# Third weight unit asked for four pairs sooner, one store for a tile's sums, loads ahead of stores, another order of the first inputs

## The chip, the cores and the metric

The kernel runs on one core of a Trainium2 chip. The metric is the time of one execution on the device in microseconds (us). The kernel before took 2228.83, 2224.96 and 2224.57 us in three runs, a median of 2224.96 us.

## What is computed

One layer of a hybrid encoder on x of 2048 rows by 1024 columns, in float32:

```python
h    = rmsnorm(x, norm_w)                       # row by row
proj = h @ w_in                                 # 1024 -> 10 groups of 1024 columns: q, ffwd, fbwd, i, ga, u, v, gb, ma, mb
y_a  = hgrn2(q, ffwd, fbwd, i, ga)              # two gated linear scans, 8 heads, norm, SiLU gate
y_b  = gelu(u) * (W_s @ layernorm(gelu(v)) + b) * silu(gb)
out  = rmsnorm(x + (sigmoid(ma)*(y_a @ w_proj_a) + sigmoid(mb)*(y_b @ w_proj_b)) @ w_out, final_norm_w)
```

The part that the change touches is the very first: h from x, and h times the 1024 columns of `w_in` that make `i`.

## The kernel before, in words

**Numbers in two halves.** A float32 operand is held as two float16 tensors, a high half and a low half (the rest). A product is three float16 products: high by high, high by low, low by high. These are the three matmuls of lines 218, 219 and 220, repeated for the eight slices of 128 of the depth.

**x.** The 2048 rows are eight pairs of two tiles of 128 rows. `x_pair(n)` makes pair n in four steps: ACT squares both tiles as they lie in `in_x` (L280, which also sums each row), POOL makes 1/sqrt of the mean and puts it on the diagonal of two 128x128 tiles (L283 to L286), PE multiplies a matrix of ones by these diagonals (L290), which spreads each row's factor over all partitions, DVE multiplies the transposed columns of x by it (L296, four times for each half of the depth), ACT rounds to the high half (L300) and DVE makes the low half (L301). Rows come by L263, transposed columns by L267. Two pairs fill one of the four `xT` tiles, which is also stored (`store(b)`, L384: two stores of 1 MB).

**Weights of i.** They come in four units of 256 columns, 1 MB each. `halves` (called through `load`) makes one: DMA of `wraw` (L188), squares on ACT (L192), a cast to bfloat16 on POOL (L196), a matmul with ones on PE, here called the norm (L200, into the one-bank tile `misc`), a power of two from it on DVE (`pow2`, L142 to L147), then for each half the high half on ACT (L207) and the low half on DVE (L208). Line 192 writes its squares, which nobody reads, into the unit's own low half.

**Pairs of i.** `i_pair(hp, n)` multiplies pair n of x by unit hp: 48 matmuls, here written (hp, n), and ACT empties the result (L448). Units 0 and 1 are run through while x is still being made, in the order of the list `seq`: (0,0) (1,0) (0,1) (1,1) (0,2) (0,3) (1,2) (1,3) (0,4) (0,5) (1,4) (1,5) (0,6) (0,7). The table `beside` says what is issued in the middle and after each of them. The pairs (1,6) and (1,7) follow as `i_late`, in `i_stage(2)`, then (2,0) to (2,7), then `i_stage(3)` with (3,0) to (3,7), then the stage `values()`. In `front()` unit 2 (the third unit) is loaded after `x_stage` has been written:

```python
self.x_stage(xr)
...
self.plan_units()
last = self.i_stage(2, self.unit(self.w_in, C_I + 2 * U, ahead=0), wu3)
```

**Sums of x.** A later stage needs four sums S1, S3, S2, S4 of blocks of x. `x_parts(p, k)` makes one of eight tiles of them, each in two steps of `self.parts`: DVE adds (L963), then ACT and DVE make the halves (L955, L956) in a tile `st`, and four stores of 256 KB put them into four arrays (L958). `st` is the single buffer `xst`, or for two of the eight the former row buffer `xt2` (shown as `xt`).

**What sets the order.** The framework's scheduler puts the instructions of each engine in one order, and each engine runs its own in that order. It follows roughly the order in which Python wrote them, with `tc.high_priority` and `tc.issue_after` for a few at the start, but an instruction can land behind some that were written later: the norm of unit 2 is written ahead of (1,6) and stands behind (1,7). All DMAs of this part are issued by the SP queue in order. They share eight semaphores in rotation, so that an issue also waits until the DMA eight issues earlier has landed. `self.make(at)` issues what a plan of units (`plan_units`) has due by the number `at`: loads, squares and scales of the weights of the `values()` stage (L1011 to L1070, L1084).

## Time and profile before

| | |
|---|---|
| median of three runs | 2224.96 us |
| the profiled execution | 2224.79 us |
| its span | 2223.1 us |
| PE busy | 2164.2 us (97%) |
| DVE, ACT, POOL busy | 1664.5, 1347.8, 334.5 us |
| first matmul of unit 2's norm (L200) | at 126.42 us |

The profile is of one execution. Idle time before an instruction stands in brackets behind it with what ended it. The lowest rate of the clock that the throttle granted to PE is 0.50, the highest 1.00; a column of the windows gives it for each stretch.

### The profile page before, as it was taken

The numbers are of one execution on the slowest core, as the hardware profiler recorded it, in microseconds if no ns is written. First come the engines' busy times: TensorE is split into PE (matmuls) and PEld (weight loads), VectorE is DVE, ScalarE is ACT, GpSimd is POOL, SyncE is SP. The second block draws the span as 40 slices with busy tenths as digits, with TensorE's granted clock in tenths as the row PEclk, the third lists the DMA queues.
The fourth block names the chain that finished last, engine by engine and source line by source line (L and its number), as shares of the span: only waits on it lengthen the run. The fifth ranks groups of instructions, "written<-read, shape, count | busy, mean of one in ns | idle before, by whom it ended". The sixth has DMA issues, their size and how long they took to land.

```text
span 2223.1 us, 35062 instructions
## 1 busy us (share of the span) xinstructions
PE 2164.2 (97%) x12654; PEld 1216.8 (55%) x12654; DVE 1664.5 (75%) x3063; ACT 1347.8 (61%) x2740; POOL 334.5 (15%) x526
## 2 busy tenths in 40 slices
PE   8979999999999999999899999999999999999998
PEld 6868444566666666666454544444445544444444
DVE  6867876688999989989677775588874744687764
ACT  6466876676877877867465564676764622344442
POOL 1125743002402202203100000000000000000011
PEclk9989999999999999999999999999999999999999
DMA  8886996768678668776742223779756675777643
GB/s 318 320 292 263 364 398 243 225 208 218 188 216 248 196 167 258 220 201 192 239 147 95 83 98 123 273 288 324 287 174 220 214 252 179 274 259 285 251 160 104
DMA packets 269449, 503.92 MB, mean 227 GB/s; under 512 B 92880, under 2 KB 154576, under 8 KB 245584
## 3 DMA queue, kind: packets, MB, share of 16 engines
q1 hardware_dynamic: 246080, 459.36, 62.2%
q10 hardware_dynamic: 23184, 42.22, 5.1%
q8 instruction: 101, 1.65, 0.3%
q14 instruction: 84, 0.69, 0.1%
HBM read 317.74 MB, written 166.99 MB: 218 GB/s over the span
## 4 chain that ended last, share of the span: by engine, by line
PE 47%; issue 3%; DVE 0%; ACT 0%; POOL 0%; POOLq 0%; ACTq 0%; DVEq 0%
PE bank L1161 46%; PE px L1491 1%; PE px L1795 0%; DVE seven L1061 0%; ACT seven L1060 0%; DVE zs L1197 0%; ACT tmp L1011 0%; POOL wsb L1016 0%; PE px L1068 0%; DVE tmp L1030 0%; DVE zs L2017 0%; POOLq L2289 0%; ACT zs L2036 0%; DVE raw L1030 0%; POOL rstd L2029 0%
## 5 line engine op out<-in xcount | busy, mean ns | idle before, releaser
L1161 PEld LDWEIGHTS <-seven 128*128 128x128 f16 x7404 | 722.6, 100 | 765.2 <-issue 7.9
L1161 PE MATMUL bank<-xT,seven 128*128 128x512 f16 x4116 | 971.4, 379 | 4.2 <-ACT zs L594 2.5
L1161 PE MATMUL bank<-seven 128*128 128x512 f16 (+1 forms) x2028 | 436.0, 378 | 0.7 <-DVE zs L2017 0.7
L1161 PE MATMUL bank<-xs,seven 128*128 128x512 f16 x1260 | 282.2, 379 | 0.0
L1197 DVE SCALAR_TENSOR_TENSOR zs<-bank,us,zs 128x512 f32<-128x512 f32 x192 | 142.5, 744 | 90.0 <-PE bank L1161 64.2
L1109 ACT ACTIVATE zs<-bank,us 128x512 f32<-128x512 f32 x192 | 130.1, 680 | 106.3 <-PE bank L1161 100.6
L1164 PEld LDWEIGHTS sc<-ff,kt 128*128 128x128 f32 x684 | 130.0, 190 | 47.8
L1205 ACT ACTIVATE zs<-zs 128x512 f32<-128x512 f32 x144 | 90.0, 626 | 99.8 <-DVE zs L1197 87.0
L1161 PE MATMUL bank<-seven,xT 128*128 128x512 f16 x672 | 146.3, 379 | 1.2 <-DVE zs L1197 1.2
L218 PE MATMUL pin<-wsplit,xT 128*128 128x256 f16 x512 | 142.2, 279 | 4.9 <-ACT wsplit L207 4.9
L1061 DVE SCALAR_TENSOR_TENSOR seven<-raw,ws,seven 128x1024 f16<-128x1024 f32 x80 | 109.4, 1395 | 49.6 <-ACT seven L1060 48.9
L220 PE MATMUL pin<-wsplit,xT 128*128 128x256 f16 x512 | 142.0, 278 | 1.1 <-DVE xT L301 1.0
L219 PE MATMUL pin<-wsplit,xT 128*128 128x256 f16 x512 | 142.2, 278 | 0.7 <-DVE wsplit L208 0.7
L1109 ACT ACTIVATE zs<-bank,su 128x512 f32<-128x512 f32 x72 | 49.0, 682 | 144.0 <-PE bank L1161 131.6
L839 ACT ACTIVATE q<-ff,e 128x64 f32<-128x64 f32 x512 | 131.5, 336 | 1.6 <-issue 0.4
L1164 PE MATMUL sc<-ff,kt 128*128 128x64 f32 (+1 forms) x684 | 119.2, 256 | 0.0
L1161 PEld LDWEIGHTS <-xT 128*128 128x128 f16 x672 | 64.6, 98 | 77.3 <-issue 1.5
L1197 DVE SCALAR_TENSOR_TENSOR zs<-bank,su,zs 128x512 f32<-128x512 f32 x72 | 53.8, 747 | 55.5 <-PE bank L1161 44.6
L1060 ACT ACTIVATE seven<-raw,ws 128x1024 f16<-128x1024 f32 x80 | 88.5, 1137 | 5.3 <-DMA kept<-seven 2.5
L1061 DVE SCALAR_TENSOR_TENSOR seven<-tmp,ws,seven 128x768 f16<-128x768 f32 x80 | 80.5, 1035 | 10.8 <-ACT seven L1060 10.4
L915 DVE SCALAR_TENSOR_TENSOR st<-st,e,pu 128x128 f32<-128x128 f32 x224 | 75.7, 338 | 5.4 <-PE pu L907 4.3
L1575 ACT ACTIVATE zs<-zs 128x512 f32<-128x512 f32 x64 | 40.0, 625 | 55.5 <-DVE zs L1963 39.3
(270 smaller groups left out, 3207.7 us busy)
## 6 DMA issues: line engine op xcount, KB each, us to landing
xT<-x SPq DMA_DIRECT2D x71, 1024.0 KB, 7.1
raw<-in_w_in_dram SPq DMA_DIRECT2D x38, 1024.0 KB, 7.3
seven<-kept SPq DMA_DIRECT2D x15, 1792.0 KB, 9.2
kept<-seven SPq DMA_DIRECT2D x16, 1024.0 KB, 5.2
kept<-seven SPq DMA_DIRECT2D x16, 768.0 KB, 6.1
v<-v SPq DMA_DIRECT2D x20, 512.0 KB, 5.3
x<-xT SPq DMA_DIRECT2D x8, 1024.0 KB, 5.8
v<-zs SPq DMA_DIRECT2D x32, 256.0 KB, 8.5
```

The lines of the kernel that those rows point to most:

```text
L218: nc.tensor.matmul(ps, lh(k), rh(k), start=start and k == 0, stop=False, skip_group_check=len(ks) < KT)
L219: nc.tensor.matmul(ps, lh(k), rl(k), start=False, stop=False, skip_group_check=len(ks) < KT)
L220: nc.tensor.matmul(ps, ll(k), rh(k), start=False, stop=k == KT - 1, skip_group_check=len(ks) < KT)
L839: self.nc.scalar.activation(out=q0[:, at], in_=ff[:, at], func=AF.Copy, scale=e8[:, n, b:b + 1])
L915: nc.vector.scalar_tensor_tensor(out=sn, in0=st, scalar=e8[:, n, last:last + 1], in1=pu[:, n, :], op0=ALU.mult, op1=ALU.add)
L1060: nc.scalar.activation(out=out[0], in_=src, func=AF.Copy, scale=s)
L1061: nc.vector.scalar_tensor_tensor(out=out[1], in0=src, scalar=s, in1=out[0], op0=ALU.mult, op1=ALU.subtract)
L1109: self.reads["act"] = self.nc.scalar.activation(out=t, in_=ps, func=AF.Copy, scale=su)
L1161: nc.tensor.matmul(ps, lhs(x, k), rhs(y, k), start=start and not (k or n), stop=k == 3 and n == 2, skip_group_check=True)
L1164: self.fill.pop(0)()
L1197: self.reads["dve"] = self.nc.vector.scalar_tensor_tensor(out=more, in0=ps, scalar=su, in1=more, op0=ALU.mult, op1=ALU.add)
L1205: self.nc.scalar.activation(out=out, in_=more, func=func)
```

## The change

1. **Third unit.** `third()`, in the middle of the pair at entry 10 of `seq`, (1,4), loads unit 2 (DMA, squares, cast); the rest of it (norm, power of two, halves) is written where it was, by `unit()` after `x_stage`. The squares of this unit go into a free piece of a lent buffer (`junk`) and no longer into the unit's low half, which has the place of a unit that PE still reads.
2. **One store a tile.** The four sums lie in one array `x_sums_d[p]`, and `x_parts` stores its tile with one DMA of 1 MB; the old names are views of it.
3. **Loads ahead of stores.** The loads of x's pairs 4 to 7 are issued one or two pairs of `seq` sooner, and the four `store(b)` are issued after the entries 6, 7, 9 and 12 of `seq` where it was 3, 4, 8 and 10.
4. **First inputs.** Unit 0's norm is written after x's first high half; unit 1's norm and scaling come in the middle of the first pair's matmuls (`proj_tm` with `by_quads`), not in their first quarter; the spreading matmul L290 is ordered behind the one of line 102, and the first step of pair 1 behind the high half of unit 0 and not behind its squares.
5. In `i_stage(2)` the plan's work is issued before `i_late`'s pair and not after it.

```diff
@@ scale_x
-            nc.tensor.matmul(pb, self.ones[0:1, :], m1, start=True, stop=True)
+            self.spread = nc.tensor.matmul(pb, self.ones[0:1, :], m1, start=True, stop=True)
@@ halves(self, w, c0, junk=None)
         for h in range(2):
-            self.w_square = nc.scalar.activation(out=quads(wt[:, 1], h), in_=quads(raw, h), func=AF.Square,
-                                                 accum_out=ss[:, h:h + 1])
+            out = quads(wt[:, 1], h) if junk is None else junk.rearrange("p (a n) -> p a n", a=2)
+            nc.scalar.activation(out=out, in_=quads(raw, h), func=AF.Square, accum_out=ss[:, h:h + 1])
@@ proj_tm
-                if j and between and not m:
+                if between and (j and m is None or m and not j):
                     between()
@@ x_pair
-        nc.tensor.matmul(r.rearrange("p (n t) -> p n t", t=P), self.ones, diag, start=True, stop=True)
+        with self.tc.issue_after(self.spread.ins):
+            nc.tensor.matmul(r.rearrange("p (n t) -> p n t", t=P), self.ones, diag, start=True, stop=True)
@@ x_stage
             next(pairs[0])
-            next(wi)
+            next(pairs[0])
+            hi = self.x_hi
             busy(6, self.raws[0][:, 0, 1, 1, 0:P])
-            next(pairs[0])
-            unit(0, partial(next, wi))
+            with tc.issue_after(hi.ins):
+                next(wi)
+                unit(0, partial(next, wi))
...
+        def third():
+            got = self.load(*self.todo[0], junk=lent[1][:, 3072:].bitcast(F16))
+            self.made.append((self.todo.pop(0), got))
...
-            with tc.issue_after(self.w_square.ins):
+            with tc.issue_after(self.w_hi.ins):
                 next(pairs[n])
-                  3: (go(3, 2), go(3, 2) + fetch(4) + [partial(store, 0)]),
-                  4: (part, part + go(4) + fetch(5) + [partial(store, 1)]), 5: (go(4, 2), go(4, 2) + go(5)),
-                  6: (go(5, 2), go(5, 2) + fetch(6)), 7: (part + go(6) + fetch(7), part + [self.decays]),
-                  8: (go(6, 2), go(6, 2) + go(7) + [partial(store, 2)]), 9: (go(7, 2), go(7, 2)),
-                  10: (part, part + [partial(store, 3)]), 11: (part, part), 12: (part, part), 13: (part, part)}
+                  3: (go(3, 2), go(3, 2) + fetch(5) + go(4) + [partial(self.x_load, 6)]),
+                  4: (part, part + go(5) + [partial(rows, 6), partial(self.x_load, 7)]),
+                  5: (go(4, 2), go(4, 2) + [partial(rows, 7)] + go(6)),
+                  6: (go(5, 2), go(5, 2) + go(7) + [partial(store, 0)]),
+                  7: (part, part + [self.decays, partial(store, 1)]),
+                  8: (go(6, 2), go(6, 2)), 9: (go(7, 2), go(7, 2) + [partial(store, 2)]),
+                  10: (part + [third], part), 11: (part, part), 12: (part, part + [partial(store, 3)]), 13: (part, part)}
@@ i_stage
             for n, f in enumerate(self.i_late):
+                self.make(2 * n - 36)
                 f()
-                self.make(2 * n - 36)
@@ x_parts
-        for n, part in enumerate((S1, S3, S2, S4)):
-            nc.sync.dma_start(out=self.x_d[p][part][:, k], in_=st[:, n])
+        nc.sync.dma_start(out=self.x_sums_d[p][:, :, k], in_=st)
```

The instructions of each engine in their order show what this moves. On PE, the norm of unit 2 before, between the last matmul of (1,7) (L220) and the first of (2,0) (L218):

```order
L220 LDWEIGHTS xT
L220 MATMUL pin<-wsplit,xT 128x256
L200 LDWEIGHTS ones_70
L200 MATMUL misc<-wsb,ones_70 128x1
L200 LDWEIGHTS ones_70
L200 MATMUL misc<-wsb,ones_70 128x1
L218 LDWEIGHTS xT
L218 MATMUL pin<-wsplit,xT 128x256
```

With the change the norm stands two pairs sooner, between (0,7) and (1,6), and 96 matmuls lie between it and (2,0). The norm of unit 3 (the fourth unit) stands inside (2,4), 16 matmuls from its start; before it stood right behind (2,3).

On ACT with the change, from the squares of unit 2 (L193, which was L192), through its high halves (L207), to the squares of unit 3 (the last row); L459 empties the pairs, L966 makes sums of x (it was L955), L1021 and L1070 belong to the weights of the next stage:

```order
L193 ACTIVATE lent,wss<-wraw 128x1024
L966 ACTIVATE xt_261<-xraw 128x512
L966 ACTIVATE xt_261<-lent 128x3x512
L459 ACTIVATE vt<-pin 128x512
L966 ACTIVATE xst<-xraw 128x512
L207 ACTIVATE wsplit<-wraw,ws 128x2x512 x2
L966 ACTIVATE xst<-lent 128x3x512
L459 ACTIVATE vt<-pin 128x512 x2
L966 ACTIVATE xst<-xkept 128x512
L966 ACTIVATE xst<-lent 128x3x512
L459 ACTIVATE vt<-pin 128x512
```

The high halves of unit 2, which stood behind all the sums of x but one, now stand between the two conversions of the sixth tile of sums. After these rows come, on ACT, six squares of the next weights (L1021), the conversions of the eighth tile of sums, two scalings (L1070) and then the squares of unit 3:

```order
L459 ACTIVATE vt<-pin 128x512
L966 ACTIVATE xst<-xkept 128x512
L966 ACTIVATE xst<-lent 128x3x512
L1070 ACTIVATE seven<-raw,ws_1687 128x1024 x2
L193 ACTIVATE wsplit,wss<-wraw 128x2x512 x2
```

Before, the squares of unit 3 came behind the eighth tile's conversions too, with one square pair of L1011 between them and no scaling.

On SP with the change, the stretch with unit 2's load (L188); L385 stores xT, L968 the sums, L466 the results of i:

```order
L466 DMA i_2_151<-vt 128x1024
L385 DMA x_0_143<-xT 128x4096
L385 DMA x_2_144<-xT 128x4096
L188 DMA wraw<-in_w_in_dram 128x2048
L968 DMA x_sums_147<-xt_261 512x1x1024
L466 DMA i_2_155<-vt 128x1024
L968 DMA x_sums_147<-xst 512x1x1024
L385 DMA x_7_146<-xT 128x4096
L968 DMA x_sums_148<-xt_261 512x1x1024
```

Before, the same load stood behind six tiles of sums:

```order
L455 DMA i_3_158<-vt 128x1024
L958 DMA x_1_148<-xst 128x1024
L958 DMA x_4_151<-xst 128x1024
L958 DMA x_5_152<-xst 128x1024
L958 DMA x_6_153<-xst 128x1024
L188 DMA wraw<-in_w_in_dram 128x2048
L1084 DMA raw<-in_w_in_dram 128x2048
```

It moved ahead of six of the eight stores of sums.

More of the change, by code (lines that the diff above doesn't have):

```diff
@@ L170, in step, with load @@
             self.made.append((self.todo[0], self.load(*self.todo.pop(0))))
-    def load(self, w, c0):
-        halves = self.halves(w, c0)
+    def load(self, w, c0, junk=None):
+        halves = self.halves(w, c0, junk)
         next(halves)
@@ L182, in load, with halves @@
         return rest
-    def halves(self, w, c0):
+    def halves(self, w, c0, junk=None):
         nc, sm = self.nc, self.sm
@@ L206, in halves @@
         for h in range(2):
-            nc.scalar.activation(out=quads(wt[:, 0], h), in_=quads(raw, h), func=AF.Copy, scale=s)
+            self.w_hi = nc.scalar.activation(out=quads(wt[:, 0], h), in_=quads(raw, h), func=AF.Copy, scale=s)
             nc.vector.scalar_tensor_tensor(out=quads(wt[:, 1], h), in0=quads(raw, h), scalar=s, in1=quads(wt[:, 0], h),
@@ L399, in x_stage @@
             next(pairs[0])
-            next(wi)
+            next(pairs[0])
+            hi = self.x_hi
             busy(6, self.raws[0][:, 0, 1, 1, 0:P])
-            next(pairs[0])
-            unit(0, partial(next, wi))
+            with tc.issue_after(hi.ins):
+                next(wi)
+                unit(0, partial(next, wi))
             next(pairs[0])
             next(pairs[0])
-        with tc.issue_after(self.x_hi.ins):
+        with tc.issue_after(hi.ins):
             wi = self.load(*self.todo[0])
@@ L414, in first @@
         def first(n):
-            with tc.issue_after(self.w_square.ins):
+            with tc.issue_after(self.w_hi.ins):
                 next(pairs[n])
-        beside = {0: ([partial(unit, 1, wi), partial(first, 1)], fetch(3)), 1: (go(1, 4), go(2)), 2: (go(2, 2), go(2, 2) + go(3)),
-                  3: (go(3, 2), go(3, 2) + fetch(4) + [partial(store, 0)]),
-                  4: (part, part + go(4) + fetch(5) + [partial(store, 1)]), 5: (go(4, 2), go(4, 2) + go(5)),
-                  6: (go(5, 2), go(5, 2) + fetch(6)), 7: (part + go(6) + fetch(7), part + [self.decays]),
-                  8: (go(6, 2), go(6, 2) + go(7) + [partial(store, 2)]), 9: (go(7, 2), go(7, 2)),
-                  10: (part, part + [partial(store, 3)]), 11: (part, part), 12: (part, part), 13: (part, part)}
+        beside = {0: ([partial(unit, 1, wi), partial(first, 1)], fetch(3)), 1: (go(1, 4), go(2)),
+                  2: (go(2, 2), go(2, 2) + go(3) + fetch(4)),
+                  3: (go(3, 2), go(3, 2) + fetch(5) + go(4) + [partial(self.x_load, 6)]),
[5 more added lines that the diff above has]
+                  10: (part + [third], part), 11: (part, part), 12: (part, part + [partial(store, 3)]), 13: (part, part)}
         for m, (hp, n) in enumerate(seq):
@@ L2219, in run @@
         self.kept, self.zscale, self.zsums, self.rot = {}, {}, {}, [(0, 1, 2), (0, 1, 2)]
-        self.x_d = [[self.dram.tile([P, 4, 2, SEG], F16, name=f"x_{p}_{c}") for c in range(8)] for p in range(2)]
+        self.x_d = [[self.dram.tile([P, 4, 2, SEG], F16, name=f"x_{p}_{c}") if c in (A11, A12, A21, A22) else None
+                     for c in range(8)] for p in range(2)]
+        self.x_sums_d = [self.dram.tile([P, 4, 4, 2, SEG], F16, name=f"x_sums_{p}") for p in range(2)]
+        for p in range(2):
+            for n, part in enumerate((S1, S3, S2, S4)):
+                self.x_d[p][part] = self.x_sums_d[p][:, n]
         self.i_d = [[self.dram.tile([P, 4, U], F32, name=f"i_{hp}_{b}") for b in range(NSEG)] for hp in range(2)]
```

## The prediction

> **What bounds the kernel now.** I read the page's busy times first, then the windows of three stretches, then the waits of PE in the first stretch, row by row.
>
> ```profile
> span 2223.1 us, 35062 instructions
> PE 2164.2 (97%) x12654; PEld 1216.8 (55%) x12654; DVE 1664.5 (75%) x3063; ACT 1347.8 (61%) x2740; POOL 334.5 (15%) x526
> 0.00:140.00 140.00, 110.23 (x889) 94.03 (x890) 100.84 (x167) 74.98 (x105) 24.92 (x38) 0.89 0.86 322
> 140.00:350.00 210.00, 209.86 (x1368) 130.43 (x1366) 161.16 (x230) 159.36 (x243) 108.19 (x73) 1.00 0.84 329
> 350.00:2223.10 1873.10, 1844.08 (x10402) 992.39 (x10400) 1402.52 (x2667) 1113.47 (x2393) 201.37 (x415) 1.00 0.64 208
> ```
>
> A window's row gives its bounds and length, the busy time of PE, weight loads, DVE, ACT and POOL, the granted clock of PE, the DMA engines' share and GB/s. PE is busy 97% of the span. In the first 140 us it idles 140.00 - 110.23 = 29.8 us and its clock averages 0.89; from 140 to 350 it idles 0.14 us in 210. So the kernel is bound by PE, and its start is not. The change touches only the start, so what it saves there shifts everything after, as long as the PE-bound stretch stays full.
>
> Where the start loses time:
>
> ```profile
> 27.08 0.70 PE L290 MATMUL xps<-lent,ones 128*128 128x256 f32 x2 [3.03 <-POOL lent L286]
> 75.25 0.70 PE L290 MATMUL xps<-lent,ones 128*128 128x256 f32 x2 [2.77 <-POOL lent L286]
> 83.78 0.70 PE L290 MATMUL xps<-lent,ones 128*128 128x256 f32 x2 [1.36 <-POOL lent L286]
> 126.42 0.19 PE L200 MATMUL misc<-wsb,ones 128*128 128x1 bf16 x2 [9.18 <-POOL wsb L196]
> 131.48 1.23 PE L218 MATMUL pin<-wsplit,xT 128*128 128x256 f16 x5 [4.88 <-ACT wsplit L207]
> 133.40 0.37 PE L219 MATMUL pin<-wsplit,xT 128*128 128x256 f16 x1 [0.69 <-DVE wsplit L208]
> 76.10:79.50 3.40, 3.40 (x18) 2.43 (x17) 3.11 (x8) 2.06 (x4) 0.00 (x0) 0.50 1.02 401
> 82.90:86.30 3.40, 2.52 (x21) 2.17 (x22) 2.14 (x6) 0.47 (x1) 0.83 (x1) 1.00 0.98 405
> 131.50:137.50 6.00, 5.30 (x25) 3.62 (x25) 6.00 (x4) 4.00 (x6) 2.28 (x2) 0.50 1.00 418
> ```
>
> The brackets hold the idle time and its releaser. Unit 2's preparation costs PE 9.18 + 4.88 + 0.69 = 14.8 us, and then 6.0 us at half clock, worth 3.0. The factors of x's pairs 6 and 7 cost 2.77 + 1.36 = 4.1, and 3.4 us at half clock, worth 1.7. Pair 1's factors cost 3.03.
>
> **Third unit.** Its load was asked at 116.61 and its squares ended the wait:
>
> ```profile
> 116.61 0.45 SPq L188 DMA_DIRECT2D wraw<-in_w_in_dram  x1
> 123.65 1.06 ACT L192 ACTIVATE wsplit<-wraw 128x1024 f16<-128x1024 f32 x1 [0.58 <-DMA wraw<-in_w_in_dram]
> 85.83 0.60 ACT L448 ACTIVATE vt<-pin 128x512 f32<-128x512 f32 x1 [3.23 <-PE pin L220]
> 91.07 0.60 ACT L448 ACTIVATE vt<-pin 128x512 f32<-128x512 f32 x1 [0.96 <-PE pin L220]
> 96.31 0.60 ACT L448 ACTIVATE vt<-pin 128x512 f32<-128x512 f32 x1 [2.67 <-PE pin L220]
> wraw<-in_w_in_dram SPq DMA_DIRECT2D x4, 1024.0 KB, 8.5
> 130.28 2.19 ACT L207 ACTIVATE wsplit<-wraw,ws 128x1024 f16<-128x1024 f32 x2 [2.93 <-DVE ws L147]
> 107.26 1.76 DVE L956 TENSOR_TENSOR xt<-lent,xt 128x1536 f16<-128x1536 f32 x1 [1.60 <-ACT xt L955]
> 109.05 0.69 DVE L963 TENSOR_TENSOR lent<-xraw 128x512 f32<-128x512 f32 x1
> 43.70:109.02 65.32, 61.19 (x535) 53.38 (x534) 53.63 (x89) 33.34 (x44) 6.39 (x9) 0.97 0.84 319
> DVE xraw L296 <- PE xps L290: 4.5, 3, 2.0
> ```
>
> A pair takes 96.31 - 91.07 = 5.24 us. I place all that follows 6.7 us sooner than before (the next two parts: 4.1 + 1.7 + 0.9). The load now stands on SP behind the store of (0,5), emptied at 85.83 - 6.7 = 79.1; with three issues it is asked at about 82, and by its median of 8.5 us is there at 90.5. ACT takes the squares around (0,6)'s emptying, ending at about 97.5. (0,7) ends two pairs after (1,5), at 96.3 - 6.7 + 2 x 5.24 = 100.0: the norm waits for nothing, with 2 us to spare. (1,6) and (1,7) then cover 10.5 us, to 110.5.
>
> In that cover DVE is the narrow place. Its power of two stands behind the low halves of the fifth tile of sums, which ended at 109.02. Of the 65.3 us before, 53.6 were work. What goes of its 11.7 idle: 3.3 to 6, from its waits for PE (4.5 in all) and for ACT behind them, and 0.9 from the front. So it is there at 102.5 to 104.8; with four small operations among three sums of about 0.7 the scale is out at 105.7, two high halves of 1.1 end at 107.9, the second low half at 109.5. The first half is wanted at 110.5. Even the late end leaves nearly 1 us. I take the whole 14.8 + 3.0. If the cover fails by d, PE pays d, no more than before.
>
> **Loads ahead of stores.** Pair 6's rows were asked late, behind stores:
>
> ```profile
> 60.44 2.49 SPq L263 DMA_DIRECT2D xt<-in_x_dram  x2
> 68.91 1.06 ACT L280 ACTIVATE xT<-xt 128x1024 f16<-128x1024 f32 x1 [0.17 <-DMA xt<-in_x_dram]
> ```
>
> Now these loads stand on SP ahead of the first sums' store, and the squares of pairs 6 and 7 are written two entries of `seq` sooner, two pairs or 10.5 us, against waits of 2.77 and 1.36. I count 4.1 and, as no stall precedes it, the 1.7 of clock. The stores moved behind (`store(b)`) are read only by later stages; what they can delay is on SP, the result stores, and the load of unit 2, counted above.
>
> **First inputs.** (0,0) still waits for x's high half and unit 0's scale. Unit 1's preparation comes a little sooner, so that half of (1,0), 24 matmuls or 2.6 us, can run ahead of L290.
>
> ```profile
> 25.35 1.68 POOL L286 TENSOR_TENSOR lent<-ident,xss 128x256 f32<-128x256 f32 x1
> 28.30:31.70 3.40, 3.40 (x19) 2.42 (x17) 3.40 (x9) 3.40 (x7) 1.50 (x3) 0.50 0.95 337
> ```
>
> POOL's diagonal, which ended the wait at 27.03, comes about 1.1 later, since pair 1's squares now stand behind unit 0's second high half on ACT (1.1, half of its 2.19). PE reaches L290 at 26.7, so the wait of 3.03 falls to about 1.5. Of the 1.5 saved I count 0.9, because pair 1's high halves then queue behind the same ACT work. The bounds: -1.1 (nothing runs ahead) and +2.6 (all of it counts), and the 1.7 of half clock at 28.30, if it goes. The plan's work issued ahead of `i_late` costs nothing on PE: it is loads and squares, on SP and ACT.
>
> **One store a tile, and the new wait.** Four issues become one, eight times.
>
> ```profile
> 112.55 4.01 SPq L958 DMA_DIRECT2D x<-xst  x4
> 121.07 0.63 ACT L955 ACTIVATE xst<-xkept 128x512 f16<-128x512 f32 x1 [3.21 <-DMA x<-xst]
> 98.90 1.48 ACT L955 ACTIVATE xst<-lent 128x1536 f16<-128x1536 f32 x1 [1.36 <-DVE lent L963]
> x<-xT SPq DMA_DIRECT2D x8, 1024.0 KB, 5.8
> x<-xst SPq DMA_DIRECT2D x23, 256.0 KB, 4.9
> raw<-in_w_in_dram SPq DMA_DIRECT2D x4, 1024.0 KB, 9.1
> ```
>
> `xst` is one buffer, so ACT's next conversion waits for the landing: 121.07 - 112.55 = 8.5 us after the first of four issues. For a single 1 MB store the trace has no row; 4.9 (a quarter of the size) and 8.5 (all four) bound it, and 5.8, a store of the same size from xT, is nearest. I take 5.8.
>
> Behind these conversions in ACT's order stand the squares of the fourth unit, and its norm stands on PE 16 matmuls into (2,4), now at 110.5 + 4 x 5.24 + 1.75 = 133.2. The sixth store is asked at about 111.4 (the second low half at 109.5, then 1.76 for the sums' low halves), the next weights right behind it, there 9.1 later, at 120.6. From then ACT is full: six squares at about 1.1, two emptyings of 0.6 and three small copies of 0.1 (8.1, to 128.7), two conversions (0.63 and 1.48, 2.1), two scalings and two squares at 1.1 (4.4): 135.2, and the cast about 0.4 more. So PE waits 135.6 - 133.2 = 2.4, say 2.5, from 0 (all of it hidden by a load 2.5 sooner) to 5 (one 2.5 later). A stall of 2.77 was followed by 3.4 us at half clock, one of 1.36 was not (clock 1.00 at 82.90); 2.5 is nearer the first, so 1.7 on top.
>
> The Trainium skill ("TensorE: Matmul & The Clock Gate", HAM oscillation) states the rule that PE should have no idle gap over about 3.4 us. By it a stall of 2.5 would cost 2.5 alone, and the time would be lower by 1.7. Here 2.77 was enough for half clock, so the trace disagrees, and the measurement decides.
>
> **Later.** From 140 on the order is the same on each engine but for some rows up to 350. There PE works alone only if the others keep up:
>
> ```profile
> 182.40:221.10 38.70, 38.70 (x354) 33.85 (x353) 36.65 (x35) 26.30 (x34) 24.21 (x14) 1.00 0.64 249
> 219.19 1.93 DVE L1061 SCALAR_TENSOR_TENSOR seven<-tmp,vs,seven 128x768 f16<-128x768 f32 x2
> 219.09 2.75 PE L1161 MATMUL bank<-seven,xT 128*128 128x512 f16 x12
> ```
>
> DVE has 2 us of idle in these 38.7. Its last half for the stage `values()` ends at 221.1, when PE has begun it (219.09); by the order PE reads that half behind 24 of these matmuls, at 0.22 each 5.2 us, so 3 us are to spare. The chain begins with an event of PE and shifts with it. Only weights that come later against PE, which no longer stands some 10 us while they land, could upset it; I count nothing.
>
> **The sum.** Gains 14.8 + 3.0 + 4.1 + 1.7 + 0.9 = 24.5; losses 2.5 + 1.7 = 4.2; net 20.3. The profiled execution took 2224.79 us (the span 2223.1 and 1.7 around it), the median is 2224.96. 2224.79 - 20.3 = 2204.5.
>
> **The rivals.**
>
> *The stall moves to the fourth unit.* With the stores landing at 9.1 (the weights' figure, a little over the 8.5 of four small ones) the sixth and seventh each come 3.3 later, and ACT's work behind them: a stall of 2.5 + 6.6 = 9.1, and 1.7 of clock. Gain 24.5 - 10.8 = 13.7: 2211.1. For it: DMA share 0.86 to 1.00 in this stretch. Against: the 1 MB store's own 5.8.
>
> *The next stage takes some back.* If the weights there are late by those 10 us against PE and only 3 are covered, PE waits 7 and loses 1.7 at half clock: 20.3 - 8.7 = 11.6, 2213.2. For it: DVE is full at 182 to 221. Against: 36.65 of 38.70 was enough before without a wait.
>
> *The early load gains nothing* (the change doesn't do what it says): held back on SP, or the power of two late on DVE, so that PE waits as long before unit 2 as it did. Then 24.5 - 17.8 = 6.7 is left: 2218.1. For it: 2 us to spare at the norm, nearly 1 at the halves. Against: a delay of 1 costs 1, not 15.
>
> *Slower: the single store lands late.* One mechanism: a 1 MB store out of one buffer holds ACT, which is in order, three times: before unit 2's high halves (landing of the fourth tile), before the seventh and before the eighth tile's conversions, and behind these the fourth unit. By landing L, the first has about 5.5 us of cover beyond 5.8; the other two make the fourth unit late by 2L - 11.2 and what the first lost. At L = 14: 16.8 + 2.7, with about 5 of half clock after three stalls 24.5, the whole gain. So 14 us decides; at L = 17, 22.8 + 5.7 + 5 = 33.5, and 2233.8. Against: no store here had more than 8.5 for this megabyte.
>
> **How the numbers follow.** Chances: forecast 0.62, fourth unit 0.14, next stage 0.08, nothing from the early load 0.07, late store 0.09. About 0.2% (4.4 us) is what a measurement of this kernel can tell from no change. The first three are faster, the fourth (2218.1) for about 0.05 of 0.07; the rest of it and 0.01 of the last lie within: faster 0.89, same 0.03, slower 0.08. The forecast's own range is 2198.5 to 2210: down by the fourth unit's 4.2 and the front's 1.7; up by the front's 2.0, 2.5 of the fourth unit's stall and 1 of DVE's thin cover. The whole range goes down to 2197.0, with the front's clock too, and up to 2214.0, so that the first two rivals are in; 0.16 of the chance is left out above.
>
> **What would show it.** No wait over 1 us at L200 or L218 around 100 and 110 us, and a clock of 1.00 there; no wait at L290 for pairs 6 and 7; one wait of 0 to 5 us at L200 inside (2,4); landings of the sums' stores near 6 us; no PE wait from 180 to 225. Wrong if these stores land at 9 us or more, if DVE's power of two for unit 2 starts after 105, or if the 24.5 appear before 140 and PE idles later.

## The result, and the profile after

The changed kernel took 2205.97 us, the median of four runs (2202.51 to 2207.75), and the kernel before, on the same chip, 2226.02 us (four runs). The ratio is 0.9907, with a 95% interval of 0.9889 to 0.9924: 20.7 us less, between 17 and 25. The forecast was 2204.5 us, in a range of 2197.0 to 2214.0. The profiled execution took 2207.17 us, 17.6 less than the profiled execution before (2224.79).

The page's first lines and three windows of the changed kernel, the columns as before:

```profile
span 2205.4 us, 35017 instructions
PE 2161.6 (98%) x12654; PEld 1216.1 (55%) x12654; DVE 1665.7 (76%) x3063; ACT 1347.2 (61%) x2740; POOL 338.0 (15%) x526
0.00:130.00 130.00, 118.53 (x1016) 104.62 (x1017) 98.11 (x171) 78.79 (x116) 24.84 (x39) 0.99 0.89 333
130.00:350.00 220.00, 215.00 (x1318) 126.35 (x1316) 178.88 (x247) 167.49 (x251) 119.35 (x85) 0.99 0.89 341
350.00:2205.40 1855.40, 1828.12 (x10324) 985.11 (x10322) 1388.73 (x2647) 1100.92 (x2374) 193.79 (x403) 1.00 0.64 208
```

PE's idle time in the start fell from 29.8 to 11.5 us, and the clock there rose from 0.89 to 0.99. New is the idle time from 130 to 350: 5.0 us where it was 0.1; 1.24 of it is the wait for `zs` that stood at 364, behind the window, in the kernel before. The last long window idles 27.3, nearly what it did (29.0), of which that wait was a part. So the gain is in the start, as forecast, and a part of it came back right behind.

PE's waits of the changed kernel, row by row (lines after the change stand 1 to 11 higher: L291 was L290, L302 L301, L459 L448, L966 L955, L1021 L1011, L1028 L1018, L1078 L1068, L1171 L1161), and two windows behind them:

```profile
28.52 0.70 PE L291 MATMUL xps<-lent,ones 128*128 128x256 f32 x2 [0.89 <-POOL lent L286]
34.06 0.28 PE L220 MATMUL pin<-wsplit,xT 128*128 128x256 f16 x1 [1.35 <-DVE xT L302]
100.55 0.19 PE L200 MATMUL misc<-wsb,ones 128*128 128x1 bf16 x2 [1.69 <-POOL wsb L196]
136.94 0.19 PE L200 MATMUL misc<-wsb,ones 128*128 128x1 bf16 x2 [2.90 <-POOL wsb L196]
28.50:32.00 3.50, 3.48 (x28) 2.95 (x28) 2.74 (x7) 2.93 (x6) 1.50 (x3) 1.00 0.85 240
137.00:140.40 3.40, 3.40 (x19) 2.44 (x19) 3.37 (x13) 3.40 (x6) 0.00 (x0) 0.52 0.84 325
```

The 14.8 us before unit 2 are gone, and so are the waits for pairs 6 and 7. Behind (0,0), four waits of more than half a microsecond are left up to 140. The one at 136.94 is the fourth unit's norm, forecast at 133.2 with 2.4 us and half clock behind it: it stands at 134.04 with 2.90 us, and 3.4 us at 0.52 follow. The one at 100.55, at unit 2's norm, had been forecast as none.

Why that one is there, from SP's row of the load, ACT's first square of it, and the window between:

```profile
78.81 0.91 SPq L385 DMA_DIRECT2D x<-xT  x2
...
81.08 2.53 SPq L385 DMA_DIRECT2D x<-xT  x2
83.66 1.24 SPq L188 DMA_DIRECT2D wraw<-in_w_in_dram  x1
97.58 1.06 ACT L193 ACTIVATE lent<-wraw 128x1024 f16<-128x1024 f32 x1 [0.41 <-DMA wraw<-in_w_in_dram]
83.60:97.60 14.00, 14.00 (x131) 12.54 (x130) 11.32 (x22) 6.28 (x9) 0.00 (x0) 1.00 1.01 386
```

The load was asked 1.7 us later than I placed it and took 13.8 us where I had used the median of 8.5. Four stores of xT, 1 MB each, were asked in the five microseconds ahead of it (the first two rows), and the DMA engines were full until it landed (share 1.01).

What the fourth unit waited for, on ACT:

```profile
118.25 0.63 ACT L966 ACTIVATE xst<-xkept 128x512 f16<-128x512 f32 x1 [6.27 <-DMA x_sums<-xst]
...
121.35 1.06 ACT L1021 ACTIVATE junk<-raw 128x1024 f16<-128x1024 f32 x1 [0.61 <-DMA raw<-in_w_in_dram]
130.48 0.63 ACT L966 ACTIVATE xst<-xkept 128x512 f16<-128x512 f32 x1 [0.83 <-DMA x_sums<-xst]
134.47 1.04 ACT L193 ACTIVATE wsplit<-wraw 128x1024 f16<-128x1024 f32 x1
x_sums<-xst SPq DMA_DIRECT2D x6, 1024.0 KB, 5.4
```

The next weights landed at 121.35 (forecast 120.6), ACT then had only 0.83 us of idle up to the squares at 134.47 (forecast 133.0), and the 1 MB stores landed after 5.4 us (forecast 5.8).

At the start of `values()`, ACT's squares of a weight, the small copy behind them, the norm on PE that reads it, and two rows of DVE's work on the weights:

```profile
199.83 1.06 ACT L1021 ACTIVATE junk<-raw 128x1024 f16<-128x1024 f32 x1 [3.68 <-DMA raw<-in_w_in_dram]
...
202.20 0.20 ACT L1028 ACTIVATE wsb<-wss 128x2 bf16<-128x2 f32 x1
202.55 0.19 PE L1078 MATMUL px<-wsb,ones 128*128 128x1 bf16 x2
179.00 4.11 DVE L1071 SCALAR_TENSOR_TENSOR seven<-raw,vs,seven 128x1024 f16<-128x1024 f32 x2
...
187.52 4.11 DVE L1071 SCALAR_TENSOR_TENSOR seven<-raw,vs,seven 128x1024 f16<-128x1024 f32 x2
PE px L1078 <- ACT wsb L1028: 0.8, 3, 0.3
```

PE reads the copy 0.15 us after its end and does not wait; three later norms of this kind wait 0.8 us in all. The time to spare at this place is used up.

### The profile page after: what moved, and what is told of

Same layout as the page of the kernel before. It is cut to its first block, busy times and chain, and to the rows that moved or that the text cites. A ratio compares the mean times of both kernels' runs of the same rounds, so it can differ in the third digit from the quotient of the medians.

```text
span 2205.4 us, 35017 instructions
## 1 busy us (share of the span) xinstructions
PE 2161.6 (98%) x12654; PEld 1216.1 (55%) x12654; DVE 1665.7 (76%) x3063; ACT 1347.2 (61%) x2740; POOL 338.0 (15%) x526
## 4 chain that ended last, share of the span: by engine, by line
PE 44%; issue 3%; DMA 2%; DVE 1%; ACT 0%; POOL 0%; SPq 0%; POOLq 0%; DVEq 0%; ACTq 0%
PE bank L1171 43%; PE px L1501 1%; DMA mg<-zs 1%; DVE seven L1071 1%; DMA raw<-mg 0%; PE px L1805 0%; DMA seven<-kept 0%; DVE zs L1207 0%; DMA zs<-mb 0%; ACT seven L1070 0%; DVE tmp L973 0%; ACT tmp L1021 0%; POOL wsb L1026 0%; DVE zs L1973 0%; DVE zs L1961 0%
## 5 line engine op out<-in xcount | busy, mean ns | idle before, releaser
L1171 PEld LDWEIGHTS <-seven 128*128 128x128 f16 x7404 | 722.8, 100 | 767.0 <-issue 10.3
L1171 PE MATMUL bank<-xT,seven 128*128 128x512 f16 x4116 | 972.1, 380 | 4.8 <-ACT zs L605 2.5
L1171 PE MATMUL bank<-seven 128*128 128x512 f16 (+1 forms) x2028 | 436.1, 378 | 1.0 <-DVE zs L2027 0.7
L1171 PE MATMUL bank<-xs,seven 128*128 128x512 f16 x1260 | 282.2, 379 | 0.0
L1215 ACT ACTIVATE zs<-zs 128x512 f32<-128x512 f32 x144 | 90.0, 627 | 102.8 <-DVE zs L1207 90.8
L1171 PE MATMUL bank<-seven,xT 128*128 128x512 f16 x672 | 146.5, 379 | 1.2 <-DVE zs L1207 1.2
L220 PE MATMUL pin<-wsplit,xT 128*128 128x256 f16 x512 | 140.2, 274 | 2.2 <-DVE xT L302 2.2
L219 PE MATMUL pin<-wsplit,xT 128*128 128x256 f16 x512 | 140.2, 274 | 0.9 <-DVE wsplit L208 0.9
L218 PE MATMUL pin<-wsplit,xT 128*128 128x256 f16 x512 | 140.4, 274 | 0.0
L1171 PEld LDWEIGHTS <-xT 128*128 128x128 f16 x672 | 64.6, 98 | 77.2 <-issue 1.5
L1070 ACT ACTIVATE seven<-raw,ws 128x1024 f16<-128x1024 f32 x80 | 88.3, 1138 | 6.3 <-DVE ws L147 2.8
L1071 DVE SCALAR_TENSOR_TENSOR seven<-tmp,ws,seven 128x768 f16<-128x768 f32 x80 | 82.1, 1056 | 10.8 <-ACT seven L1070 10.4
L1040 POOL TENSOR_TENSOR tmp<-raw 128x512 f32<-128x512 f32 x40 | 59.6, 1490 | 108.3 <-DVE seven L1071 40.1
```

The costliest lines, as they stand in the source:

```text
L218: nc.tensor.matmul(ps, lh(k), rh(k), start=start and k == 0, stop=False, skip_group_check=len(ks) < KT)
L219: nc.tensor.matmul(ps, lh(k), rl(k), start=False, stop=False, skip_group_check=len(ks) < KT)
L220: nc.tensor.matmul(ps, ll(k), rh(k), start=False, stop=k == KT - 1, skip_group_check=len(ks) < KT)
L1070: nc.scalar.activation(out=out[0], in_=src, func=AF.Copy, scale=s)
L1071: nc.vector.scalar_tensor_tensor(out=out[1], in0=src, scalar=s, in1=out[0], op0=ALU.mult, op1=ALU.subtract)
L1171: nc.tensor.matmul(ps, lhs(x, k), rhs(y, k), start=start and not (k or n), stop=k == 3 and n == 2, skip_group_check=True)
```

## The experiments

Each kernel was timed against the kernel before in five rounds; ratios are to that. Beside the ratio, two places on PE help: the start of the last matmul of (3,7), where the stage with i ends, and the end of a wait that every kernel has some 145 us later in `values()` (the first matmul behind a wait of about 1 us for DVE's `zs`).

The fifth part of the change, the plan's work issued ahead of `i_late`'s pair, was undone in no run, so its worth is not shown.

| kernel | last matmul of (3,7) | behind the wait in `values()` | ratio, 95% interval |
|---|---|---|---|
| before | 218.98 | 364.33 | 1 |
| changed | 199.85 | 346.02 | 0.9907 (0.9889 to 0.9924) |
| changed, no early third unit | 213.52 | 358.87 | 0.9967 (0.9954 to 0.9980) |
| changed, four stores | 200.34 | 346.11 | 0.9902 (0.9887 to 0.9916) |
| changed, loads as before | 201.79 | 353.79 | 0.9932 (0.9919 to 0.9945) |
| changed, front as before | 201.19 | 348.38 | 0.9918 (0.9906 to 0.9931) |
| before, early third unit alone | 211.18 | 358.45 | 0.9962 (0.9950 to 0.9975) |
| third sooner still | 199.48 | 345.39 | 0.9923 (0.9910 to 0.9936) |
| fourth sooner | 194.59 | 347.55 | 0.9918 (0.9905 to 0.9931) |
| both | 199.43 | 349.93 | 0.9925 (0.9912 to 0.9937) |
| third's DMA sooner | 200.54 | 346.45 | 0.9903 (0.9888 to 0.9918) |
| third mb weight later | 200.20 | 350.05 | 0.9916 (0.9902 to 0.9929) |
| fourth sooner, mb later | 201.08 | 350.39 | 0.9917 (0.9903 to 0.9930) |
| DMA and fourth sooner, mb later | 196.56 | 347.22 | 0.9909 (0.9894 to 0.9923) |

Where two ratios differ by 0.0025 or less their intervals overlap; there the two places of the trace, of one execution each, carry the reading. They are no finer than about 1 us: pair 3's spreading matmul, which is the same work in the eleven kernels with the changed front, starts between 40.90 and 41.91 in them. And from the place in `values()` to the end of the span the executions take between 1856.4 and 1862.6 us, so a single profiled execution says less of the whole time than of these places.

### One part undone

**Without the early third unit.**

```diff
-                  10: (part + [third], part), 11: ...
+                  10: (part, part), 11: ...
```

> The changed kernel with the third unit loaded where it was before (after the last x work), all else as changed. My theory: the early load carries most of the gain. PE then waits again at unit 2's norm and halves, about 15 us after (1,7), with 3 us of half clock behind it; the 1.7 us at the norm behind (0,7) and the fourth unit's stall with its clock (2.9 + 1.6) go. 15 + 3 - 1.7 - 4.5 = 11.8 us more than the changed kernel, about 2218. Rival: the gain comes from the relieved queue (fewer stores, loads ahead of them), and the load was never the limit: within 3 us of the changed kernel, 2206 to 2209, with a wait of under 5 us before (2,0).

Measured 2220.18 us, ratio 0.9967: 0.0060 more than the changed kernel, 13.3 us. PE's waits behind (1,7):

```profile
121.92 0.19 PE L200 MATMUL misc<-wsb,ones 128*128 128x1 bf16 x2 [12.95 <-POOL wsb L196]
125.91 1.23 PE L218 MATMUL pin<-wsplit,xT 128*128 128x256 f16 x5 [3.79 <-ACT wsplit L207]
127.83 0.37 PE L219 MATMUL pin<-wsplit,xT 128*128 128x256 f16 x1 [0.70 <-DVE wsplit L208]
125.00:135.00 10.00, 8.40 (x52) 6.22 (x52) 4.45 (x3) 3.14 (x5) 5.95 (x4) 0.64 1.01 374
```

That is 17.4 us of waiting. By the mean of 0.64, 7.2 of the 10 us from 125 on are at half clock; 0.9 of them lie in the wait, which leaves 6.3, worth 3.1 by the prediction's way of counting. The load was the limit, and the rival falls. The wait is longer than before (14.8), since PE was there 8 us sooner and the load was asked only 5 us sooner, at 111.36 for 116.61: without the early load, this place took part of what the other edits save.

**Four stores a tile.**

```diff
-        nc.sync.dma_start(out=self.x_sums_d[p][:, :, k], in_=st)
+        for n, part in enumerate((S1, S3, S2, S4)):
+            nc.sync.dma_start(out=self.x_d[p][part][:, k], in_=st[:, n])
```

> The changed kernel with the four 256 KB stores a tile in place of one of 1 MB. My theory: the single store matters only through the landing that ACT's next conversion waits for, 5.4 us against about 8.5: the conversions of the eighth tile come some 3 us later and with them the fourth unit's norm: its stall grows from 2.9 to about 6, 2209. Rival: the 24 more issues also hold SP in front of the third unit's load, the norm behind (0,7) waits 5 us or more instead of 1.7, and it is 2212 or more. Other rival: the ACT work between (six squares) covers the later landing, no change (within 1 us).

Measured 2206.32 us, ratio 0.9902: no difference, as the other rival had it. ACT in this kernel:

```profile
117.69 0.63 ACT L966 ACTIVATE xst<-xkept 128x512 f16<-128x512 f32 x1 [7.61 <-DMA x_sums<-xst]
129.98 0.62 ACT L966 ACTIVATE xst<-xkept 128x512 f16<-128x512 f32 x1
```

The seventh tile's conversion waits longer for its buffer (7.61 for 6.27 us) and comes no later on the clock, as this kernel was 1.9 us ahead there; the eighth tile's waits for nothing, since ACT's six squares cover the landing. I had counted the landing as added to ACT's work, and it lies beside it. The fourth unit's norm still waits: 3.82 us, as PE came there 1.4 us sooner, and it starts at 136.49 for 136.94. The single store is worth nothing that can be measured in this kernel.

**Loads and stores of x as before.** The table `beside` of before, with `third` at its place in entry 10.

> The changed kernel with x's loads and its four 1 MB stores in the order of before (the third unit's early load stays at its place). My theory: the waits for pairs 6 and 7 come back, 4.1 us with 1.7 of half clock: 5.8 more, about 2212. Less by up to 1.7 if the stores, now sooner, leave the way free for the third unit's load, whose landing took 13 us in the changed kernel. Rival: the wait for pairs 6 and 7 is hidden in the later wait at the third unit's norm, so that the order is worth nothing: within 1 us of the changed kernel.

Measured 2211.91 us, ratio 0.9932: 0.0025 more, 5.5 us, the size that I expected, but on another path. PE:

```profile
73.61 1.18 PE L291 MATMUL xps<-lent,ones 128*128 128x256 f32 x2 [3.27 <-POOL lent L286]
82.87 0.70 PE L291 MATMUL xps<-lent,ones 128*128 128x256 f32 x2 [1.87 <-POOL lent L286]
209.08 0.19 PE L1075 MATMUL px<-wsb,ones 128*128 128x1 bf16 x2 [3.67 <-ACT wsb L1025]
108.70 0.97 SPq L188 DMA_DIRECT2D wraw<-in_w_in_dram  x1
```

The waits for pairs 6 and 7 are back, 5.1 us, with 3.4 lost at half clock (0.83 from 70 to 90, a loss of 0.17 x 20). But the waits at 100.55 and 136.94 are gone, so (3,7) ends only 1.9 us later. The rest is lost in `values()`: a wait of 3.67 us for the squares of a weight, with half clock behind it. The undoing is not a clean one: it also moves the load of the fourth unit, which is asked at 108.70 here (the last row) and at 123.36 in the changed kernel. So it stands ahead of the first weights of the next stage, which are asked at 117.53 for 113.45, and ACT emptied (3,4) 6.2 us later. This is the rival "the next stage takes some back" seen in a run, but how much of the 5.5 us the loads and stores of x alone are worth, it doesn't say.

**Front as before.** The order of the first inputs, line 102's ordering and the place of `between` in `proj_tm`.

> The changed kernel with the order of the first inputs of before (unit 0's norm ahead of x's high half, unit 1's in the first quarter, no ordering of the spreading matmul). My theory: pairs (1,0) to (1,1) were emptied 0.8 to 2.8 us sooner, so about 2 us come back: 2208. Rival: a later wait absorbs it (the load of the third unit, asked at a fixed place on SP, lands no sooner for an earlier front): within 1 us of the changed kernel.

Measured 2208.64 us, ratio 0.9918, 0.0011 more (2.4 us), with overlapping intervals. In the trace the wait of 3.03 at L290 is back, and at the end of (3,7) it is 1.3 us behind, in `values()` 2.4. Pair 3's spreading matmul starts at 43.14, and at 41.12 in the kernel with four stores, whose trace begins alike (the first one at 9.32 in both). So the front is worth the theory's 2 us where it stands. Behind it the rival is seen too: the wait of 1.69 at unit 2's norm is gone, but the fourth unit's has grown from 2.90 to 4.47. The ratios alone would not show it.

### The early load alone, on the kernel before

The three pieces that the early load needs (`junk` in `load` and `halves`, the function `third`, and `third` in entry 10), nothing else.

> The kernel before with the third unit's early load alone (squares into the free piece, load asked in the middle of (1,4)); loads, stores and front as before. My theory: the parts add up. Undoing the early load cost 13.3 us, so alone it should bring 13 to 15 us: 14.8 + 3.0 less a fourth unit's stall of about 3 with some half clock: 2212 to 2215 beside 2227. Rival: it needs the loads ahead of the stores, since SP in the order of before asks for it too late: a wait of over 5 us at unit 2's norm and a gain under 8 us, 2219 or more.

Measured 2219.19 us, ratio 0.9962: 8.5 us less than before. My expectation was wrong, and the rival's time came, though not by its path:

```profile
75.10 1.22 PE L290 MATMUL xps<-lent,ones 128*128 128x256 f32 x2 [2.83 <-POOL lent L286]
84.41 0.91 PE L290 MATMUL xps<-lent,ones 128*128 128x256 f32 x2 [2.43 <-POOL lent L286]
147.54 0.19 PE L200 MATMUL misc<-wsb,ones 128*128 128x1 bf16 x2 [4.20 <-POOL wsb L196]
147.00:155.00 8.00, 7.46 (x46) 5.67 (x46) 5.62 (x14) 8.00 (x15) 0.18 (x1) 0.62 0.80 300
```

There is no wait at unit 2's norm, so the load came in time (asked at 88.91). But the fourth unit's norm waits 4.2 us and loses some 2.8 more at half clock (0.63 from 147.50, where the wait ends, to 155), and the waits for pairs 6 and 7 have grown from 4.1 to 5.3 us. Half clock now follows the second of these too (0.54 from 84.50 to 87.90). The same part is worth 13.3 us with the others there and 8.5 without: they are not a sum, because each shifts what the next wait is.

### What is left to gain in the start

**Third unit sooner still**, with `third` in the middle of entry 8, (0,4), in place of entry 10.

> The changed kernel with the third unit's load asked two entries sooner still, in the middle of (0,4), so that it stands ahead of two of the 1 MB stores of xT. My theory: the load took 13.8 us in the changed kernel because these stores (1 MB each) were in front of it in full DMA engines; asked sooner it is there before its squares' turn and the 1.7 us wait at the norm behind (0,7) goes. PE's part to the end of (3,7) shrinks by 1.7. Whether the end does too is open: 1.7 less (about 2205) if later stages follow PE, nothing (2206 to 2207) if a wait of the next stage takes it.

Measured 2208.99 us. `third` carries the squares too, and at entry 8 they are written into the piece that holds the factors of x's pair 7 before PE has read them. So this kernel leaves out pair 7's own factors, and PE waits for the squares:

```profile
91.75 0.67 PE L291 MATMUL xps<-lent,ones 128*128 128x256 f32 x2 [3.57 <-ACT lent L193]
```

The wait at unit 2's norm is gone, as expected, with this one in its place. What the sooner load is worth can't be read from it; the next run asks for the load alone.

**Third unit's DMA sooner**, its squares where they were:

```diff
+        def ask():
+            w, c0 = self.todo[0]
+            self.early = self.wu.tile([P, KT, U], F32, name="wraw", tag="wsplit")
+            nc.sync.dma_start(out=self.early.rearrange("p k n -> p (k n)"), in_=w[c0 // U])
...
-                  8: (go(6, 2), go(6, 2)), 9: ...
+                  8: (go(6, 2) + [ask], go(6, 2)), 9: ...
```

> The changed kernel with the DMA of the third unit alone asked in the middle of (0,4), ahead of two 1 MB stores of xT; its squares stay where they were written, behind the last use of the free piece. Theory (a floor): the weights of the next stage are made by DVE, ACT and POOL on their own clock up to about 201 us, and the changed kernel just meets it. Then the 1.7 us wait at the norm behind (0,7) goes, (3,7) ends about 1.7 sooner at most, and the end does not move: 2206 to 2208. Rival: PE alone bounds, and the time falls by 1.7 to about 2205.

Measured 2206.29 us, ratio 0.9903, the changed kernel's within the intervals. The load is asked at 78.14, ahead of two of the four stores, and is there at 89.7, after 11.5 us. The wait at unit 2's norm is gone, and the next one has grown by nearly as much:

```profile
136.71 0.19 PE L201 MATMUL misc<-wsb,ones 128*128 128x1 bf16 x2 [4.35 <-POOL wsb L197]
```

It ends at 136.71 for 136.94, and (3,7) ends no sooner (200.54 for 199.85), since half clock follows for longer (0.59 from 136.70 to 143.00). So the time is the one that the theory gave, but the run doesn't test it: PE gained nothing that the next stage could have taken. That the stores ahead of it delayed the load is borne out by all these kernels together: it landed after 13.5 to 14.0 us in the five where all four stores were asked in the 6 us ahead of it, after 10.5 to 11.5 in the four with two ahead, after 11.4 with the front of before, where two were asked just ahead and two some 6 us sooner, and after 5.6 and 5.9 in the two where none was asked in the 7 us ahead (the early load alone; loads and stores as before).

**Fourth unit sooner.**

```diff
+            self.wt = wt
+            self.step(1)
             for n, f in enumerate(self.i_late):
                 self.make(2 * n - 36)
...
-                if n in (0, 3):
+                if n == 3:
                     self.step(1)
```

> The changed kernel with the fourth unit's load written ahead of i_late, so that its squares stand on ACT ahead of the six squares of the next weights, and not behind them and the eighth tile's conversions. My theory: ACT's order made the stall at the fourth unit's norm; it goes with its half clock, 2.9 + 1.6 = 4.5: about 2202 if the later stages follow PE. Rival: the weights of the next stage, now later on ACT, make a wait of 3 us or more there (as with the loads in the order of before, 3.7 us behind (3,7)), and the time stays within 1.5 us of the changed kernel. Other rival: the stall is the conversion's wait for the store, then a wait of 2 us or more stays at the fourth unit's norm.

Measured 2208.67 us, ratio 0.9918. On PE up to (3,7) my theory held: no wait at the fourth unit's norm, and the last matmul at 194.59 for 199.85, 5.3 us sooner. Of this nothing arrives. PE and ACT behind (3,7):

```profile
196.33 1.89 PE L1173 MATMUL bank<-seven,xT 128*128 128x512 f16 x8 [0.61 <-DVE seven L1073]
201.75 0.19 PE L1080 MATMUL px<-wsb,ones 128*128 128x1 bf16 x2 [3.53 <-ACT wsb L1030]
199.13 1.06 ACT L1023 ACTIVATE junk<-raw 128x1024 f16<-128x1024 f32 x1 [4.01 <-DMA raw<-in_w_in_dram]
198.00:206.00 8.00, 4.47 (x14) 1.62 (x13) 3.76 (x9) 3.57 (x7) 5.92 (x5) 0.66 1.01 422
```

4.1 us of waiting, and behind it 2.8 lost at half clock (0.50 from 201.70 to 207.40). ACT's squares of that weight start at 199.13; in the changed kernel they start at 199.83, and PE came to their norm 4.3 us later (202.55 for 198.22) and did not wait. So the changed kernel had no time to spare here, and its stall of 2.90 at the fourth unit costs nothing: it stands ahead of a later bound that takes what its removal gives.

**Both of the first and the third of these.**

> Both of the last two together. My theory: 1.7 + 4.5 = 6.2 us less up to the end of (3,7), and about 2200 if it is passed on. Rival: a wait of 3 us or more in the next stage takes most of it: 2204 to 2207.

Measured 2211.26 us, with the same squares over pair 7's factors (a wait of 3.55 us at L291) and 2.92 us behind (3,7).

### Is the later bound DVE's?

The stage `values()` needs four weights, which POOL, ACT and DVE make in turn, one in about 8.5 us (187.52 - 179.00 on DVE in the changed kernel), up to some 202 us. Ahead of them DVE scales the third mb weight, which is needed much later. Moving that behind them should take work off the chain:

```diff
-            b = (-29, -26, -17.9)[n] if n < 3 else ...
-            load = (-36, -35.9, -27.5, -9.9)[n] if n < 4 else ...
-            ... ((-34, -33, -23)[n] if n < 3 else b - 3.4, m.square) ...
+            b = (-29, -26, -5)[n] if n < 3 else ...
+            load = (-36, -35.9, -13, -9.9)[n] if n < 4 else ...
+            ... ((-34, -33, -9)[n] if n < 3 else b - 3.4, m.square) ...
```

> The changed kernel with the third mb weight (of those made for later stages) due 13 steps later in the plan, behind the four weights that the next stage needs, so that about 9 us of DVE's work come off the chain ahead of that stage. Floor theory: the changed kernel has no wait of over 0.3 us at the start of that stage, so without earlier work on PE there is nothing to gain: within 1.5 us of the changed kernel. Rival: the moved work makes DVE late inside the stage, 3 us or more slower.

> The fourth unit's load written ahead of i_late, as in the run where (3,7) ended 5.3 us sooner and the time did not fall, now with the third mb weight behind the next stage's weights. Floor theory: the floor is 9 us lower, the wait of 3.5 us behind (3,7) goes, and the 4.5 to 5.3 us reach the end: about 2202. Rival: the lost time had another cause (DMA, POOL), then a wait of 2 us or more stays behind (3,7) and the time stays at 2206 or more.

> All three: third unit's DMA asked sooner, fourth unit's load sooner, third mb weight later. Floor theory: 1.7 + 4.5 less, about 2200. Rival as before: 2206 or more.

Measured 2210.97, 2208.85 and 2206.71 us (ratios 0.9916, 0.9917, 0.9909). All three expectations missed by their theory: the first lies neither within 1.5 us of the changed kernel nor 3 above it, and the other two came out at the times of their rivals. Alone, the edit makes a wait of 2.40 us behind (3,7) that was not there. With the fourth unit sooner, waits for squares on ACT come in other places; the two largest of the last kernel:

```profile
191.39 0.19 PE L1086 MATMUL xps<-wsb,ones 128*128 128x1 bf16 x2 [2.65 <-ACT wsb L1036]
201.20 0.19 PE L1086 MATMUL px<-wsb,ones 128*128 128x1 bf16 x2 [1.78 <-ACT wsb L1036]
```

(3,7) ends 3.3 us sooner than in the changed kernel, and at the place in `values()` it is 1.2 us behind.

These three runs are no clean test of the bound, since the edit makes a wait of its own. ACT, and behind it PE, in the kernel with the third mb weight later alone:

```profile
202.09 1.15 ACT L1070 ACTIVATE seven<-raw,ws 128x1024 f16<-128x1024 f32 x1 [5.24 <-DVE ws L147]
203.15 1.04 ACT L1021 ACTIVATE junk<-raw 128x1024 f16<-128x1024 f32 x1
205.46 0.19 PE L1078 MATMUL px<-wsb,ones 128*128 128x1 bf16 x2 [2.40 <-ACT wsb L1028]
```

The moved weight's scaling on ACT waits 5.24 us for its power of two from DVE, and the squares for PE's norm stand behind it; in the other two the same scaling waits 2.84 us. And less work was moved than I had counted: in the changed kernel DVE's scaling of the third mb weight takes 4.4 us (165.27 to 169.61), not 9.

What set the bound in the two kernels without this edit can be read from their rows. First the changed kernel, then the one with the fourth unit sooner:

```profile
186.92 0.68 DVE L461 SCALAR_TENSOR_TENSOR vt<-pin,vt 128x512 f16<-128x512 f32 x1
187.62 0.32 SPq L466 DMA_DIRECT2D v<-vt  x1
189.30 1.15 SPq L1094 DMA_DIRECT2D raw<-in_w_in_dram  x2
185.88 0.68 DVE L461 SCALAR_TENSOR_TENSOR vt<-pin,vt 128x512 f16<-128x512 f32 x1
186.59 0.32 SPq L466 DMA_DIRECT2D v<-vt  x1
188.26 1.16 SPq L1096 DMA_DIRECT2D raw<-in_w_in_dram  x2
```

DVE makes the low half of a result of i (L461) between its scalings of the weights. SP's store of that result waits for it, and the load of a later weight stands behind the store on SP. The load lands 10.5 and 10.8 us after it was asked, and ACT's squares start at 199.83 and 199.13. So the weight whose norm PE computes there comes only about 1 us sooner where PE is 5.3 us sooner: in these two kernels the bound goes from DVE's order over SP's order and the load to ACT. DVE's work is a link of it, as I had argued, but not the only one. No run here takes a single link away, so which of them would have to move first stays open. No kernel here beats the changed one by more than its interval.

## Why the prediction was right, point by point

- **Third unit: held, but for one term.** The 14.8 + 3.0 us are gone and DVE's narrow cover sufficed: no wait at the halves of unit 2. It was as narrow as feared: DVE's power of two started at 105.09, just past the 105 that the prediction had named as a sign of being wrong. (The early end of its range for this, 102.5, should be 102.1 by its own terms; nothing hangs on it.) Wrong was the landing: 13.8 us and not 8.5, so that the 2 us to spare at the norm became a wait of 1.69. The price of the stores moved behind the loads was set at nothing, with the load of unit 2 named as what they can delay; that delay was the one to work out.
- **Loads ahead of stores: held.** 4.1 + 1.7 forecast, and both waits are gone. Undoing it costs 5.5 us, but mostly in the next stage and with the fourth unit's load moved as well, so that figure is no measure of the two waits.
- **First inputs: too small.** 0.9 forecast. The wait at L290 fell from 3.03 to 0.89, its half clock (1.7) went, and a wait of 1.35 at 34.06 for pair 1's low half came. (0,7) ended at 98.85 and not at 100.0, so the front brought about 2.0, as the kernel with the front of before shows by its pair 3; undoing it cost 2.4 by the medians.
- **One store a tile: held in its landing, not in its worth.** 5.4 us for the 5.8 taken. That it decides the fourth unit's stall was wrong: with four stores a stall of 3.82 is there that ends no later, and it goes when the fourth unit's squares stand sooner in ACT's order.
- **Fourth unit: held, its half clock with some luck.** 2.5 + 1.7 forecast at 133.2; 2.90 + 1.6 at 134.04. The clock fell after a wait of 2.90, as the wait of 2.77 had let expect; 1.69 at 100.55 was not followed by it (1.00 in the window from 98.90). But a wait of 2.65 in the last kernel was not followed by it either (1.00 from 191.40 to 195.40), and one of 1.87 was, with the loads as before (0.58 from 83.40 to 86.80). So the length of a wait doesn't decide it in these runs, and a stall of 2.5 could have gone either way. The Trainium skill ("TensorE: Matmul & The Clock Gate", HAM oscillation) has the rule that PE should have no idle gap over about 3.4 us. The traces don't agree with that limit: the waits of 1.87, 2.77 and 2.90 were shorter, and half clock followed each.
- **Later: nothing forecast, 0.8 lost.** PE's shift was 19.1 us at the last matmul of (3,7) and 18.3 at the wait in `values()`, with 0.8 us in three waits for squares of weights there. The 3 us to spare that I had counted were used up. What failed is the step that the chain behind PE begins with an event of PE and shifts with it: with the fourth unit sooner, PE shifted by 5.3 us more and the chain by about 1.
- **The sum.** 20.3 forecast; 24.5 of gains became 25.6 with the front's 2.0 (4.1 + 1.7 + 17.8 + 2.0), less 1.7 at unit 2's norm, 4.5 at the fourth unit's and 0.8 later: 18.6, where the profiled execution shows 17.6 and the medians 20. The errors partly cancel (1.1 too little at the front; 1.7, 0.3 and 0.8 of losses missed), and that the medians lie within 0.3 us of the forecast is luck: their interval is 17 to 25.
- **The rivals.** The early load was worth 13.3 us, so that it gains nothing fell. The stall at the fourth unit was 2.90 and not 9.1, and the late single store fell too (5.4 us against its 14). The next stage taking gain back did not decide the result, but it is what comes next: PE waits for weights in `values()` with the loads as before (3.67 us) and with the fourth unit sooner (4.1 us).

## What to carry to other kernels

A wait that PE has ahead of a full stage is worth its length only as long as the next chain of the other engines does not end first; here some 19 us fitted, and the next 5.3 brought nothing, so look for the engine that is full in the next stage and for its time to spare before removing another wait. A transfer's price is that of the moment at which it is asked: a median of 8.5 us was 13.8 behind four stores of 1 MB, and 5.6 where none was just ahead. And a part's worth measured by undoing it (13.3 us) is not what it brings alone (8.5 us).

## What the runs showed that was not expected

A longer wait for a buffer was fully hidden by unrelated work behind it in the same engine's order (7.61 us for 6.27, no change). Half clock followed a wait of 1.87 us and not one of 2.65. An edit that moved only loads and stores of x also moved a weight's load by 15 us in the scheduler's order (108.70 for 123.36). And PE's small matmul for a weight of a much later stage, 0.19 us in itself, held PE for 3.5 us when its squares were late: its place in PE's order makes it a wait for everything behind it.
